# Hybrid gMLP and attention trunk on one core: the fourth quadrant of direct pairs moved into the fifth product's bank, seven-product pairs spread over the slab, four of them in layer B

## The chip, the cores and the metric

The kernel runs on one core of a Trainium2 chip. The metric is the device time of one launch in microseconds. Five engines work side by side and meet through semaphores: TensorE (PE in the profile; its weight loads are PEld), VectorE (DVE), ScalarE (ACT), GpSimd (POOL) and SyncE (SP), which here issues all DMAs.

## The reference, cut to what matters

Two residual layers on 256 tokens of width 2048, all in fp32. Nearly all the work is in four weight matrices that are read once each.

```python
def mixer_a(h, w_in, ln_g, ln_b, w_s, b_s, w_out):       # w_in 2048 x 12288, w_out 4096 x 2048
    p = h @ w_in
    uv = jax.nn.gelu(p[..., :2 * A_WIDTH], approximate=False)
    u, v = uv[..., :A_WIDTH], uv[..., A_WIDTH:]
    z = p[..., 2 * A_WIDTH:]
    v = layer_norm(v, ln_g, ln_b)
    mixed = jnp.einsum('gts,bnsgc->bntgc', ws, vc) + b_s.T[None, None, :, :, None]
    return (u * mixed.reshape(b, s, A_WIDTH) * jax.nn.silu(z)) @ w_out

def mixer_b(h, w_in, w_out, slopes):                     # w_in 2048 x 20480, w_out 2048 x 2048
    p = h @ w_in                                         # q, k, v of three groups, and z
    # three dilated causal window attentions, 16 heads of 128, merged by softmax denominators
    return (o * jax.nn.silu(z)) @ w_out

# reference(): x + mixer_a(rms_norm(x)), then x + mixer_b(rms_norm(x)), then a last rms_norm
```

## The kernel before, in words

**Splitting.** TensorE multiplies in a reduced fp32 form, so each fp32 operand is split into a rounded high part and a remainder. `split` (L126) does it with a ScalarE copy (L127) and a VectorE subtraction (L128). `triple` (L196) adds one 128 x 128 by 128 x 512 product to a bank of PSUM with three matmuls: high by high (L198), remainder by high (L199) and high by remainder (L200). The weights are split as they stream in: `load_pair` (L182) brings 256 rows of two chunks of 512 columns, left and right, by two DMAs of 512 KB into a `raw` tile, and the parts go to `wh` and `wl` (four buffers each, `NW`).

**Slabs and pairs.** `slab` (L202) computes 256 tokens by two chunks of columns. The 2048 rows of the sum are taken as eight pairs of blocks of 128. A pair is a 2 x 2 by 2 x 2 product of blocks: four result quadrants, (token half, chunk), called (0, L), (0, R), (1, L), (1, R). A *direct* pair costs eight products, 24 matmuls. A *seven-product* pair uses sums of blocks as Strassen's scheme does (Winograd's form): seven products, 21 matmuls. The sums of the operand are made once for a layer (`Operand.from_full`, L149). The sums of the weights, `tsum`, are made for each pair on VectorE (L247, L249, L250) and are split too, so such a pair has a split of 1536 columns of `raw` and one of 2048 columns of `tsum`, and takes two buffers of `wh` and `wl`.

The first five pairs of a slab are direct and fill four banks; then the bank of (1, R) is copied out by ScalarE (L241), and the last three pairs (`SA`, `SB`) are seven-product ones, which fill seven banks: q1, p5, p6, p7 and the three quadrants left. At the end a ScalarE copy and eight VectorE operations (L276 to L290) combine the banks into the quadrants, and `done` brings each through ScalarE to its tile. Layer A has twelve slabs: four for v, the first of them all direct because its operand is still being made, and eight for u and z. Layer B has twenty: in each of four quarters of the heads three for q and k, two for v and z. The two output projections (a_w_out two slabs of 16 pairs, b_w_out one slab of 8, then single chunks) are all direct.

**Small work.** Transposes, mixing, scores, softmax and values are put off by `later` and taken one at a time by `tick` (L116) between products, so many ticks apart. Each takes a bank of the same eight (`psp`) and must be emptied by ScalarE or VectorE before the bank serves again.

**Order.** The code is written in this order, but a scheduler moves instructions on every engine and picks buffers and banks. Each engine then runs its own list in order, and the DMAs are issued in SyncE's order.

**Buffers.** `wraw` has three `raw` tiles, `wsum` one `tsum` tile. `stp` has 23 tiles of 4 KB a partition for everything else, the layers' split operands among them.

## Time and profile before

| | |
|---|---|
| time, median of 3 runs | 1792.81 us (1789.93 to 1798.74) |
| profiled execution: time | 1792.22 us |
| its span (first to last instruction) | 1790.4 us |
| PE busy | 1754.9 us, 98% |
| PEld busy | 1443.3 us, 81% |
| DVE busy | 1385.2 us, 77% |
| ACT busy | 973.7 us, 54% |
| DMA | 337.5 MB, 188 GB/s, 57% of 16 engines |
| granted TensorE clock | 9 tenths or more in each of 40 slices |

A matmul's busy time is modelled from its start on and overlaps the next one's, so PE's share alone does not say that TensorE runs at its peak; the distance from one start to the next does. The time outside the span is 1.8 us.

### The profile page before, as it was taken

The page shows a single profiled execution, that of the slowest core. Times are in us where ns is not written, and L with a number is a line of the kernel's source. Part 1 is how long each engine was busy: PE and PEld are TensorE (multiplying, and loading weights), DVE is VectorE, ACT ScalarE, POOL GpSimd, SP SyncE. Part 2 cuts the span into 40 slices and gives each one's busy share as a digit, 9 for nine tenths or more (in the row PEclk, how much of TensorE's full clock was granted, in tenths as well). Part 3 has the DMA queues.
Part 4 walks back from the last instruction along what each step waited for, and adds up shares of the span by engine and source line. Part 5 has one row for each costly group of instructions (what it writes and reads, how often), then busy time and mean ns, then how long its engine had stood idle before and what let it go on. Part 6 is the DMA issues. An engine that isn't in the chain of part 4 may idle for free.

```text
span 1790.4 us, 21099 instructions
## 1 busy us (share of the span) xinstructions
PE 1754.9 (98%) x8185; PEld 1443.3 (81%) x8185; DVE 1385.2 (77%) x1291; ACT 973.7 (54%) x903; POOL 5.3 (0%) x9
## 2 busy tenths in 40 slices
PE   8999999999999999999999999999999999999997
PEld 7787778888887888778888888888888888888786
DVE  5688998888889554687788777887878878788743
ACT  5555455555556443555575455754457545566533
POOL 0000000000000000000000000000000000000000
PEclk9999999999999999999999999999999999999999
DMA  8655555655555775655555555555555555555662
GB/s 272 202 185 188 192 193 194 193 190 189 185 186 169 244 238 190 191 176 171 180 176 189 169 171 180 175 190 185 178 188 188 189 181 183 188 188 187 202 234 71
DMA packets 176596, 337.50 MB, mean 189 GB/s; under 512 B 10768, under 2 KB 14832, under 8 KB 176496
## 3 DMA queue, kind: packets, MB, share of 16 engines
q1 hardware_dynamic: 176496, 336.16, 57.1%
q8 instruction: 64, 1.05, 0.2%
q14 instruction: 36, 0.29, 0.0%
HBM read 330.35 MB, written 5.77 MB: 188 GB/s over the span
## 4 chain that ended last, share of the span: by engine, by line
PE 73%; DVE 13%; issue 6%; ACT 5%; DMA 2%; SPq 0%; POOL 0%; ACTq 0%; DVEq 0%; POOLq 0%
PE acc L200 23%; PE acc L199 22%; PE acc L198 22%; DVE wl L128 7%; ACT wh L127 4%; DVE tsum L247 2%; DVE tsum L250 1%; DVE tsum L249 1%; PE po L666 1%; PE po L668 1%; PE sc L596 1%; PE pp L609 1%; PE sc L590 1%; PE pm L462 1%; DMA raw<-in_b_w_in_dram 1%
## 5 line engine op out<-in xcount | busy, mean ns | idle before, releaser
L128 DVE TENSOR_TENSOR wl<-raw,wh 128x2048 fp32r<-128x2048 f32 (+2 forms) x308 | 636.5, 2068 | 121.9 <-ACT wh L127 121.8
L127 ACT CAST wh<-raw 128x2048 fp32r<-128x2048 f32 (+2 forms) x308 | 531.3, 1736 | 318.0 <-PE acc L199 192.1
L198 PE MATMUL acc<-wh,bh 128*128 128x512 f32 x980 | 395.2, 403 | 2.2 <-ACT full L171 2.2
L199 PE MATMUL acc<-wh,bl 128*128 128x512 f32 x980 | 384.5, 392 | 0.0
L200 PE MATMUL acc<-wl,bh 128*128 128x512 f32 x980 | 384.3, 392 | 0.0
L128 DVE TENSOR_TENSOR wl<-tsum,wh 128x2048 fp32r<-128x2048 f32 x93 | 213.0, 2291 | 193.1 <-ACT wh L127 193.1
L127 ACT CAST wh<-tsum 128x2048 fp32r<-128x2048 f32 x93 | 177.7, 1910 | 312.6 <-DVE tsum L250 156.1
L198 PE MATMUL acc<-wh,ah 128*128 128x512 f32 x603 | 238.8, 398 | 2.3 <-ACT ah L127 2.1
L200 PE MATMUL acc<-wl,ah 128*128 128x512 f32 x603 | 234.9, 392 | 1.5 <-DVE wl L128 1.5
L199 PE MATMUL acc<-wh,al 128*128 128x512 f32 x603 | 236.2, 392 | 0.1
L198 PEld LDWEIGHTS acc<-wh,bh 128*128 128x128 f32 x980 | 184.3, 188 | 41.0 <-ACT full L171 2.4
L200 PEld LDWEIGHTS acc<-wl,bh 128*128 128x128 f32 x980 | 184.0, 188 | 38.8
L199 PEld LDWEIGHTS acc<-wh,bl 128*128 128x128 f32 x980 | 184.5, 188 | 34.5
L200 PEld LDWEIGHTS acc<-wl,ah 128*128 128x128 f32 x603 | 113.4, 188 | 26.5 <-DVE wl L128 2.7
L198 PEld LDWEIGHTS acc<-wh,ah 128*128 128x128 f32 x603 | 113.4, 188 | 26.1 <-ACT ah L127 2.7
L199 PEld LDWEIGHTS acc<-wh,al 128*128 128x128 f32 x603 | 113.7, 189 | 23.7 <-DVE al L128 1.0
L247 DVE TENSOR_TENSOR tsum<-raw 128x1024 f32<-128x1024 f32 x93 | 113.2, 1218 | 4.0 <-DMA raw<-in_a_w_in_dram 3.1
L198 PE MATMUL acc<-wh,gh 128*128 128x512 f32 x256 | 100.1, 393 | 0.7 <-ACT gh L127 0.7
L199 PE MATMUL acc<-wh,gl 128*128 128x512 f32 x256 | 99.9, 390 | 0.4 <-DVE gl L128 0.4
L200 PE MATMUL acc<-wl,gh 128*128 128x512 f32 x256 | 98.9, 390 | 1.3 <-DVE wl L128 1.3
L198 PE MATMUL acc<-wh,bsh 128*128 128x512 f32 x240 | 94.5, 394 | 0.0
L199 PE MATMUL acc<-wh,bsl 128*128 128x512 f32 x240 | 93.6, 390 | 0.0
(197 smaller groups left out, 1976.2 us busy)
## 6 DMA issues: line engine op xcount, KB each, us to landing
raw<-in_b_w_in_dram SPq DMA_DIRECT2D x320, 512.0 KB, 4.6
raw<-in_a_w_in_dram SPq DMA_DIRECT2D x188, 512.0 KB, 4.6
raw<-in_a_w_out_dram SPq DMA_DIRECT2D x56, 512.0 KB, 4.8
raw<-in_b_w_out_dram SPq DMA_DIRECT2D x8, 1024.0 KB, 5.1
raw<-in_b_w_out_dram SPq DMA_DIRECT2D x12, 512.0 KB, 6.2
...
```

The source lines that it names most:

```text
L127: nc.scalar.copy(out=hi, in_=src)
L128: nc.vector.tensor_tensor(out=lo, in0=src, in1=hi.bitcast(F32), op=ALU.subtract)
L198: nc.tensor.matmul(acc, a[0], wh, start=start, stop=False)
L199: nc.tensor.matmul(acc, a[1], wh, start=False, stop=False)
L200: nc.tensor.matmul(acc, a[0], wl, start=False, stop=stop)
L247: nc.vector.tensor_tensor(out=tsum[:, 0:2, :], in0=raw[:, 0:1, :].broadcast_to([P, 2, CW]), in1=raw[:, 1:3, :], op=ALU.add)
L249: nc.vector.tensor_tensor(out=tsum[:, 2, :], in0=tsum[:, 0, :], in1=raw[:, 2, :], op=ALU.add)
L250: nc.vector.tensor_tensor(out=tsum[:, 3, :], in0=tsum[:, 2, :], in1=raw[:, 3, :], op=ALU.add)
L462: nc.tensor.matmul(pm[:, f, t, :], v[:, t, fs], wsT[:, i, :], start=True, stop=True)
L590: nc.tensor.matmul(sc[:, b, :], q[:, i, b * P : (b + 1) * P], k[:, i, :], start=True, stop=True)
L596: nc.tensor.matmul(sc[:, b, :], q[:, i, bs], k[:, i, bs], start=True, stop=True)
L609: nc.tensor.transpose(pt[:, j, :], Sh[:, b, j * P : (j + 1) * P], ident)
```

## The change

Three things change in `slab`.

1. A direct pair's products go to the banks of the seven-product scheme: (0, L) to p2, (1, L) to p4, (1, R) to p5. The bank p5 enters both right quadrants, so (0, R) gets what it lacks by a product with the difference of the two token halves, put into p3. No bank and no copy for (1, R) is left over, so direct and seven-product pairs can stand in any order.
2. Two strings give each pair's kind and two tuples the order in which pairs are taken. Layer A has three seven-product pairs in all twelve slabs (before: none in the first slab), taken as D D D S D S S D. Layer B has four in each slab (before: three), taken as D S D S S D S D. Once the last seven-product pair is done, `early` reads q1, p6 and p7 out, and a direct pair is still to come.
3. The operands keep the blocks that a pair needs, differences included, in tiles of 13 blocks in a pool of their own (`opp`, eight tiles). Layer A's first group of rows is made by `first_group`.

Around it: `tsum` shares the `raw` pool, now four tiles; `stp` has 11 tiles; a_w_out's operand is split in both of its slabs, a group ahead, and only the very first slab splits its first pairs in halves; v is normalised on ScalarE instead of VectorE; the last chunk's weights use `wh` and `wl`; y shares tiles with x3; 11 instead of 4 idle matmuls stand after the first transposes.

```diff
-WARM2 = 4
-NST = 23
+WARM2 = 11
+NST = 11
 NW = 4
-NRAW = 3
-
-SA = 3
-SB = 3
-LOOK = 1
+NRAW = 4
+KINDS_A, ORDER_A = "DDDSDSDS", (0, 1, 2, 3, 4, 5, 7, 6)
+KINDS_B, ORDER_B = "DSDSDSDS", (0, 1, 2, 3, 5, 4, 7, 6)
...
-    wsum = ctx.enter_context(tc.tile_pool(name="wsum", bufs=1))
+    opp = ctx.enter_context(tc.tile_pool(name="opp", bufs=8))
...
+        def sums(self, kg, f, n):
...
+                if kinds[i] == "D":
+                    h = q.rearrange("p (k t) m -> p k t m", t=NT)
+                    tt(out=sf[:, m : m + 2, :], in0=h[:, :, 0, :], in1=h[:, :, 1, :], op=ALU.subtract)
...
+                else:
+                    a11, a21, a12, a22 = (q[:, b, :] for b in range(4))
+                    for o, i0, i1 in ((0, a21, a22), (1, a11, sf[:, m]), (2, a21, a11), (3, a12, sf[:, m + 1])):
+                        tt(out=sf[:, m + o, :], in0=i0, in1=i1, op=ALU.subtract)
...
+            split(sf[:, 0:m, :], self.hi[kg][:, n : n + m, :], self.lo[kg][:, n : n + m, :])
...
-    def slab(h, w, cl, cr, dst, done, s=0, pre=None):
+    def slab(h, w, cl, cr, dst, done, pre=None, fine=0):
...
+        def eight(j):
+            if not h.seven:
+                return [((t, side), (j, t), side) for t in range(NT) for side in (L, R)]
+            return [("p2", (j, 0), L), ("p4", (j, 1), L), ("p5", (j, 1), R), ("p3", ("d", j), R)]
+        seven = (("q1", (0, 0), 0, 1), ("p2", (1, 0), 0, 3), ("p3", "s4", 0, 2), ("p6", "s2", 1, 2),
+                 ("p7", "s3", 1, 1), ("p5", "s1", 1, 0), ("p4", (1, 1), 1, 3))
...
+        def early():
+            nc.scalar.copy(out=c12, in_=acc["q1"])
+            tt(out=c22, in0=acc["p6"], in1=c12, op=ALU.subtract)
+            tt(out=c21, in0=c22, in1=acc["p7"], op=ALU.add)
...
+        for n, i in enumerate(h.order):
...
+            tsum = wraw.tile([P, 4, CW], F32, name="tsum", tag="raw")
...
+            if left["q1"] == 0:
+                early()
...
-        if n > s:
-            nc.scalar.copy(out=dst[R][:, 1, :], in_=acc.pop((1, R)))
...
-        nc.scalar.copy(out=q1, in_=acc["q1"])
-        tt(out=c11, in0=q1, in1=acc[(0, L)], op=ALU.add)
+        tt(out=c11, in0=c12, in1=acc["p2"], op=ALU.add)
         done(0, L, c11)
-        tt(out=u2, in0=acc["p6"], in1=q1, op=ALU.subtract)
-        tt(out=c21, in0=u2, in1=acc["p7"], op=ALU.add)
-        tt(out=u2, in0=u2, in1=acc["p5"], op=ALU.add)
-        if n > s:
-            tt(out=c22, in0=c22, in1=acc["p5"], op=ALU.add)
-            tt(out=c22, in0=c22, in1=c21, op=ALU.add)
-        else:
-            tt(out=c22, in0=c21, in1=acc["p5"], op=ALU.add)
+        tt(out=c12, in0=c22, in1=acc["p5"], op=ALU.add)
+        tt(out=c22, in0=c21, in1=acc["p5"], op=ALU.add)
         done(1, R, c22)
-        tt(out=c12, in0=u2, in1=acc[(0, R)], op=ALU.add)
+        tt(out=c12, in0=c12, in1=acc["p3"], op=ALU.add)
         done(0, R, c12)
-        tt(out=c21, in0=acc[(1, L)], in1=c21, op=ALU.subtract)
+        tt(out=c21, in0=acc["p4"], in1=c21, op=ALU.subtract)
         done(1, L, c21)
...
-            slab(hA, a_w_in[0], AW + c * CW, AW + (c + 1) * CW, v2, v_done, 0 if c == 0 else SA, pre)
+            slab(hA, a_w_in[0], AW + c * CW, AW + (c + 1) * CW, v2, v_done, pre, 2 if c == 0 else 0)
...
-                nc.vector.tensor_scalar(out=v[:, t, :], in0=v[:, t, :], scalar1=mv[:, t, 0:1],
-                                        scalar2=rL[:, t : t + 1], op0=ALU.subtract, op1=ALU.mult)
+                nc.scalar.activation(out=v[:, t, :], in_=v[:, t, :], func=AF.Identity, scale=rL[:, t : t + 1],
+                                     bias=mL[:, t : t + 1])
...
-            if sl == 0 and n == 0:
-                for kg in range(NCH_A - 1):
-                    gA.from_full(kg, gT[kg], False)
-            if sl == 0 and n == AW // P - 2 * KG:
-                gA.from_full(NCH_A - 1, gT[NCH_A - 1], False)
+            if n % KG == 0:
+                for kg in range(2) if n == 0 else (n // KG + 1,):
+                    if kg < NCH_A:
+                        gA.from_full(kg, gT[kg])
...
-    y = [st([P, NT, CW], f"y{c}") for c in range(NQUAD)]
+    y = x3[: NQUAD - 1] + [st([P, NT, CW], "y")]
...
-        for half in range(2):
-            wh = st([P, 2, CW], "fh", F32R)
-            wl = st([P, 2, CW], "fl", F32R)
-            split(raw[:, half * 2 : half * 2 + 2, :], wh, wl)
-            ws += [(kg * KG + half * 2 + j, wh[:, j, :], wl[:, j, :]) for j in range(2)]
+        wh, wl = new_split()
+        split(raw, wh, wl)
+        ws += [(kg * KG + j, wh[:, j, :], wl[:, j, :]) for j in range(KG)]
```

Three places show how the instructions move.

First, VectorE in a slab for q and k of the third quarter of layer B, before: the end of one slab and the first splits of the next. `wl<-raw` of 1536 columns and `wl<-tsum` belong to a seven-product pair, `wl<-raw` of 2048 columns to a direct one; `tmp`, `q` and `k` are the combination of banks; `Sh` is a head's scores.

```order
L128 TENSOR_TENSOR wl_9639<-raw_9631,wh_9638 128x1536
L599 SCALAR_TENSOR_TENSOR Sh_8712<-dm12_83,sc_9568 128x2x128
L128 TENSOR_TENSOR wl_9643<-tsum_9634,wh_9642 128x2048
L128 TENSOR_TENSOR wl_9675<-raw_9667,wh_9674 128x1536
L247 TENSOR_TENSOR tsum_9670<-raw_9667 128x1024
L249 TENSOR_TENSOR tsum_9670<-tsum_9670,raw_9667 128x512
L250 TENSOR_TENSOR tsum_9670<-tsum_9670,raw_9667 128x512
L128 TENSOR_TENSOR wl_9679<-tsum_9670,wh_9678 128x2048
L128 TENSOR_TENSOR wl_9726<-raw_9722,wh_9725 128x2048
L277 TENSOR_TENSOR q_9389<-tmp_9703,acc_9398 128x512
L279 TENSOR_TENSOR tmp_9703<-acc_9616,tmp_9703 128x512
L128 TENSOR_TENSOR wl_9767<-raw_9763,wh_9766 128x2048
```

The same engine, changed, in a slab for q and k of the same quarter: from the end of the combination into the run of two seven-product pairs and the direct pair behind it.

```order
L316 TENSOR_TENSOR q_8775<-acc_8788,q_8775 128x512
L288 TENSOR_TENSOR tsum_9251<-tsum_9251,raw_9246 128x512
L128 TENSOR_TENSOR wl_9250<-raw_9246,wh_9249 128x1536
L289 TENSOR_TENSOR tsum_9251<-tsum_9251,raw_9246 128x512
L287 TENSOR_TENSOR tsum_9293<-raw_9288 128x1024
L288 TENSOR_TENSOR tsum_9293<-tsum_9293,raw_9288 128x512
L289 TENSOR_TENSOR tsum_9293<-tsum_9293,raw_9288 128x512
L128 TENSOR_TENSOR wl_9258<-tsum_9251,wh_9257 128x2048
L128 TENSOR_TENSOR wl_9292<-raw_9288,wh_9291 128x1536
L128 TENSOR_TENSOR wl_9300<-tsum_9293,wh_9299 128x2048
L287 TENSOR_TENSOR tsum_9372<-raw_9367 128x1024
L128 TENSOR_TENSOR wl_9336<-raw_9332,wh_9335 128x2048
```

Three seven-product pairs in a row before the slab's end have become at most two in a row, with a direct pair on either side; the combination follows a direct pair.

Second, TensorE at the program's start, before: `pt` are the transposes of x (`x0` arrives in two halves of columns), `pwarm` the idle matmuls, and the first product ends the fence.

```order
L354 MATMUL pc_112<-ident_80,rows_84 128x16
L176 MATMUL pt_132<-ident_80,x0_105 128x128 x2
L176 MATMUL pt_137<-ident_80,x0_105 128x128 x2
L336 MATMUL pwarm_142<-ones_87 128x128 x4
L176 MATMUL pt_147<-ident_80,x0_105 128x128 x2
L176 MATMUL pt_152<-ident_80,x0_105 128x128 x2
L198 MATMUL acc_157<-wh_124,ah0_130 128x512
```

The same, changed:

```order
L208 MATMUL pt_139<-ident_80,x0_105 128x128 x2
L363 MATMUL pwarm_149<-ones_87 128x128 x11
L231 MATMUL acc_161<-wh_125,ah0_131 128x512
L231 MATMUL acc_165<-wh_125,ah0_131 128x512
L231 MATMUL acc_169<-wh_125,ah0_131 128x512
L232 MATMUL acc_161<-wh_125,al0_132 128x512
L233 MATMUL acc_161<-wl_126,ah0_131 128x512
```

The transposes of the second half of x0 no longer stand ahead of the first products; in the changed list they come after nine products' matmuls and one more.

Third, ScalarE where layer B ends and b_w_out begins, before (`oh0` is the first part of b_w_out's operand, read back from memory into `gl`; `vB2` and `zB` are the last slab's results):

```order
L276 COPY tmp_12108<-acc_12011 128x512
L127 CAST wh_12143<-raw_12138 128x1024
L127 CAST wh_12218<-raw_12213 128x1024
L654 ACTIVATE vB2_11428<-vB2_11428,rB_5335 128x512
L127 CAST wh_12218<-raw_12213 128x1024
L127 CAST wh_12272<-raw_12269 128x2048
L127 CAST oh0_12148<-gl_12123 128x1024
```

The same, changed:

```order
L127 CAST wh_12209<-raw_12206 128x2048
L645 COPY pT_11873<-pp_12135 128x4x128
L127 CAST wh_12259<-raw_12256 128x2048
L127 CAST wh_12311<-raw_12308 128x2048
L689 ACTIVATE vB2_11497<-vB2_11497,rB_5386 128x512
L127 CAST oh0_12214<-gl_12194 128x1024
L127 CAST oh1_12219<-gl_12195 128x1024
```

The casts of the first three pairs now stand ahead of the last slab's results, and `oh0` directly behind the first of these.

## Rows read from the trace of the kernel before

**Rows 1.** The page's first part: span, and each engine's busy time.
```profile
span 1790.4 us, 21099 instructions
PE 1754.9 (98%) x8185; PEld 1443.3 (81%) x8185; DVE 1385.2 (77%) x1291; ACT 973.7 (54%) x903; POOL 5.3 (0%) x9
```

**Rows 2.** Timeline of PE, 59 matmuls in layer B (start, duration, instruction).
```profile
998.74 0.39 PE L199 MATMUL acc<-wh,bl 128*128 128x512 f32 x1
998.74 0.19 PEld L200 LDWEIGHTS acc<-wl,bh 128*128 128x128 f32 x1
...
1011.88 0.39 PE L200 MATMUL acc<-wl,bh 128*128 128x512 f32 x1
```

**Rows 3.** Stages by windows: PE, PEld, DVE, ACT, POOL busy, instructions, PEclk, DMA.
```profile
10.83:62.57 51.74, 49.54 (x221) 39.44 (x219) 35.38 (x34) 35.46 (x49) 0.70 (x1) 0.97 0.80 276
62.57:192.40 129.83, 126.58 (x551) 102.49 (x549) 102.48 (x88) 64.07 (x48) 0.00 (x0) 1.00 0.55 180
192.40:241.16 48.76, 45.00 (x205) 36.42 (x204) 48.08 (x61) 24.18 (x21) 2.14 (x1) 1.00 0.54 178
241.16:513.67 272.51, 271.86 (x1267) 224.18 (x1266) 243.47 (x239) 156.47 (x127) 0.00 (x0) 1.00 0.58 190
559.82:743.68 183.86, 179.94 (x809) 147.82 (x809) 103.83 (x73) 85.68 (x75) 0.00 (x0) 1.00 0.67 216
743.68:1680.27 936.59, 931.01 (x4397) 765.74 (x4397) 753.11 (x694) 535.88 (x510) 1.11 (x1) 1.00 0.55 180
```

**Rows 4.** Groups by line and form: count, busy, mean ns, idle before, releaser.
```profile
L128 DVE TENSOR_TENSOR wl<-raw,wh 128x2048 fp32r<-128x2048 f32 x199 | 454.5, 2284 | 96.0 <-ACT wh L127 96.0
...
L127 ACT CAST wh<-raw 128x2048 fp32r<-128x2048 f32 x199 | 377.2, 1910 | 196.1 <-PE acc L199 93.3 <-DMA raw<-in_b_w_in_dram 37.6 <-DMA raw<-in_a_w_in_dram 21.7
...
L128 DVE TENSOR_TENSOR wl<-tsum,wh 128x2048 fp32r<-128x2048 f32 x93 | 213.0, 2291 | 193.1 <-ACT wh L127 193.1
...
L127 ACT CAST wh<-tsum 128x2048 fp32r<-128x2048 f32 x93 | 177.7, 1910 | 312.6 <-DVE tsum L250 156.1 <-PE acc L199 129.6 <-DVE wl L128 17.3
L128 DVE TENSOR_TENSOR wl<-raw,wh 128x1536 fp32r<-128x1536 f32 x93 | 163.0, 1752 | 11.1 <-ACT wh L127 11.0
L127 ACT CAST wh<-raw 128x1536 fp32r<-128x1536 f32 x93 | 137.8, 1482 | 110.5 <-PE acc L199 91.8 <-DMA raw<-in_b_w_in_dram 6.8 <-issue 6.5
...
L247 DVE TENSOR_TENSOR tsum<-raw 128x1024 f32<-128x1024 f32 x93 | 113.2, 1218 | 4.0 <-DMA raw<-in_a_w_in_dram 3.1 <-DMA raw<-in_b_w_in_dram 0.4
...
L250 DVE TENSOR_TENSOR tsum<-tsum,raw 128x512 f32<-128x512 f32 x93 | 64.0, 689 | 2.1
...
L279 DVE TENSOR_TENSOR tmp<-acc,tmp 128x512 f32<-128x512 f32 x31 | 21.2, 684 | 0.2 <-PE acc L200 0.2
...
L610 ACT COPY pT<-pp 128x512 f32<-128x512 f32 x32 | 18.6, 582 | 19.5 <-PE pp L609 19.5
```

**Rows 5.** Waits in layer B's window (743.68 to 1680.27 us): total, times, longest.
```profile
PEld acc L200 <- DVE wl L128: 8.9, 20, 0.5
```

**Rows 6.** Waits in six u and z slabs (241.16 to 513.67 us).
```profile
PEld acc L200 <- DVE wl L128: 3.6, 7, 0.7
```

**Rows 7.** Timeline of PE: pauses where stages meet (in brackets: idle before, releaser).
```profile
10.42 0.66 PE L176 MATMUL pt<-ident,x 128*128 128x128 f32 x4 [4.26 <-DMA x<-in_x_dram]
...
145.77 0.50 PE L198 MATMUL acc<-wh,ash 128*128 128x512 f32 x1 [1.62 <-ACT wh L127]
...
238.28 0.50 PE L198 MATMUL acc<-wh,ash 128*128 128x512 f32 x1 [2.79 <-ACT wh L127]
...
566.66 1.19 PE L200 MATMUL acc<-wl,gh 128*128 128x512 f32 x4 [1.33 <-DVE wl L128]
...
1680.27 1.78 PE L198 MATMUL acc<-wh,oh 128*128 128x512 f32 x4 [3.42 <-ACT oh L127]
...
1758.09 0.50 PE L198 MATMUL acc<-fh,oh 128*128 128x512 f32 x1 [2.47 <-ACT fh L127]
```

**Rows 8.** Timeline of ACT at the start: the first weight cast.
```profile
6.67 1.04 ACT L127 CAST wh<-raw 128x1024 fp32r<-128x1024 f32 x1 [1.80 <-DMA raw<-in_a_w_in_dram]
```

272 lines of the change are left out of this document (139 added, 133 removed).

## The prediction

> **What bounds the kernel now.** I read the engines' shares first, then the distance of matmuls, then the stages. TensorE is busy for 98% of the span [rows 1], but a matmul's shown time overlaps the next one's, so the share alone proves nothing. The distance does: from the first to the last of 59 consecutive matmuls in layer B are 13.14 us [rows 2], so 58 steps of 0.2266 us, though each shows 0.39 us. A direct pair (24 matmuls) thus takes 5.44 us and a seven-product pair (21) 4.76 us, if nothing waits. The 69 matmuls this change removes are judged by that distance.
>
> Then the stages [rows 3]. In layer B's 20 slabs TensorE is without work for 5.6 of 936.6 us, in six slabs for u and z for 0.6 of 272.5 us. Both are bound by TensorE. VectorE is busy there for 80.4% and 89.3%. The second number matters most: **with VectorE at 89% TensorE still does not pause.** The v slabs (62.57 to 192.40 us) and the first u and z slab pause for 3.3 and 3.8 us, the first slab for 2.2 us, and there are short pauses where stages meet [rows 7].
>
> **The change, part by part.**
>
> *Matmuls removed.* Layer B gets one more seven-product pair in each of 20 slabs, layer A three in the first slab: 23 products, 69 matmuls. At 0.2266 us: 13.6 us in layer B, 2.0 us in the first slab, 15.6 us in all. In layer B that lies on the path, since nothing but TensorE sets the pace there.
>
> *What layer B pays on VectorE and ScalarE.* A pair that becomes seven-product loses a split of 2048 columns (2.284 us) and gains a split of 1536 (1.752), one of `tsum` (2.291) and three additions (1.218 and two of 0.689) [rows 4]: 4.36 us more. One combination of the eight goes (0.684). So VectorE's work per slab rises from 753.11/20 = 37.7 to 41.3 us, while the slab falls from 46.8 to 46.2 us: **89.5% busy**, what the u and z slabs already bear. ScalarE gains 1.482 us net (a cast of 1536 columns): 26.8 to 28.3 us, 61%. The copy of (1, R) becomes that of q1, at the same price. The cover is the two splits' lead that four `wh` and `wl` buffers give; without it the 4.36 us would stand in the open, 20 times. Weight loads wait for VectorE's remainders 8.9 us in 20 slabs now [rows 5], 0.45 us a slab, and 3.6 us in 6 slabs, 0.60 a slab, where VectorE is at 89% [rows 6]. I let layer B rise to that level: 0.15 x 20 = 3 us. The bound from below is nothing (no three pairs in a row any more), from above the whole 13.6 us. Layer B: 13.6 - 3 = **-10.6 us**.
>
> *Banks.* From its second to its seventh pair a layer B slab now holds seven of eight banks, so small tiles share one; before, that was so in the last three pairs. Each of them must be emptied (0.58 us for a copy by ScalarE, [rows 4]) before the next. They come two ticks or more apart, at least four products or 2.7 us. I cost that at nothing; the six slabs for u and z, whose last three pairs already run so without a pause [rows 3], are the cover. At the slab's end the new order helps: the banks of q1, p6 and p7 are read out behind one more direct pair (5.4 us), so the next slab finds four free.
>
> *First slab.* It starts when the first cast ends, 6.67 + 1.04 us [rows 8], not after the second half of x0 (10.42 us, [rows 7]): up to 2.7 us earlier; the 11 idle matmuls stand in the gap before. Against that, VectorE's 35.4 us of 51.7 [rows 3] grow by three pairs (13.1 us), and by my estimate 2 us for operand differences (from the 1.218 us per 1024 columns): 50.5 us, nearly the whole slab. ScalarE grows by 4.4 us and, estimated likewise, 5 us, to 45 us. I set the slab's saved 2.0 us and its early start against that lag: **0**, between -4 and +6.
>
> *v slabs and first u and z slab.* Two of their pauses stand before seven-product matmuls that wait for a cast (1.62 and 2.79 us, [rows 7]), in the run of three such pairs. The run becomes single, then double. I take -2 of the 3.3 us and -1 of the 3.8 us (the normalisation of v now sits on ScalarE, which is half idle): **-3**, between -5 and +2.
>
> *Second half of the u and z work.* VectorE loses the two normalisations and one combination a slab, but TensorE does not wait for it: 0.
>
> *Layer A's output.* Two groups instead of seven are split at its start, where TensorE waits 1.33 us for one [rows 7]: **-1**. The splits made again in the second slab, 8 subtractions of 1024 columns at 1.218 us [rows 4], lie beside its slack (80 of 183.9 us are idle in that window, [rows 3]): 0; uncovered they would cost 10.
>
> *Layer B's end.* The pause of 3.42 us before b_w_out [rows 7] ends with the cast `oh0`, which stands behind the casts of the first pairs and waits for its load. In the changed list it stands right behind the first result. On SyncE's queue three loads `gl` now stand one behind the other, ahead of the fourth pair's second half; they wait for tiles of the last softmax, so a late one would hold that half up. **-2**, between -3 and +3.
>
> *Last chunk.* The pause of 2.47 us [rows 7] waits for the cast of `fh`, whose tiles come free late; the weights now take `wh` buffers as the chunk before frees them: **-2**, between -2.5 and +2.
>
> Sum: -10.6 - 3 - 1 - 2 - 2 = -18.6 us. The profiled execution took 1792.2 us, 0.6 us under the median of the runs. That gives 1773.6 and, for the median, **1774 us**.
>
> **A rule against it.** In layer B, weight loads fill 765.74 of 936.59 us, 82% [rows 3], and a load of 0.19 us per step of 0.2266 us [rows 2] can fill no more than 84%; so I count TensorE as full. The Trainium skill, "Perfetto Trace Analysis", section "Identifying the Most-Contended Engine", says that the share of time in matmuls is no measure of TensorE's headroom and that the share in weight loads is, while for VectorE occupancy is a fair one. Read plainly, TensorE then has 18% left, VectorE at 89.5% would be the most contended engine of layer B, and the 13.6 us would not be gained. That the busy share is no measure agrees with [rows 2]; that the load share shows 18% of room does not, since those steps leave at most 84% to the loads. I side with the distance.
>
> **Rivals.**
>
> *VectorE sets layer B's pace.* This is what that rule would make of it. A chain of subtractions has gaps (cast, then subtraction), and VectorE may saturate at less than 100%. For it: in the v slabs TensorE pauses with VectorE at 79% [rows 3]. Against it: the u and z slabs at 89%. At a saturation of 88% a slab takes 41.3/0.88 = 46.9 us, as now: layer B gains nothing, and the other -8 leave 1784 to 1785 us. At 87% a slab takes 47.5 us, which is +13 us and 1798.
>
> *Slower: the one spare bank.* Place: 36 small tiles in each quarter of layer B, 144 in all, of which most now go through one bank while its emptier stands behind a 2.29 us subtraction or a 1.91 us cast in its engine's list. Price: the mean wait times 144. It cancels the gain at 18.6/144 = 0.13 us, and makes the kernel slower by over 0.5% at 0.19 us. With half a copy (0.29 us) each time it is +42 - 18.6: 1816 us. For it: six of eight pairs instead of three run so, and the emptier's order was fixed without knowing real durations. Against it: the tiles' spacing.
>
> *The first slab lags.* VectorE needs 50.5 us and its first pairs wait for loads: +6 there, 1780 us. Still faster.
>
> **How the numbers follow.** 0.5% (9 us) is about what a measurement of this kernel can tell from no change: under 1783.8 is faster, over 1801.8 slower. Forecast, a lagging first slab included: 0.66, lying between 1764 and 1783, all faster. VectorE sets the pace: 0.21, from 1781 to 1800, a fifth of it (0.04) still faster, the rest the same. The spare bank: 0.13, half of the way up slower (0.11), the rest the same (0.02). So faster 0.70, same 0.19, slower 0.11. The range runs from 1763 to 1795: it leaves out the bank's case and the ends of the others.
>
> **What would show it.** Right: layer B takes about 926 us (46.3 a slab), VectorE near 89% there, matmuls still 0.2266 us apart, and weight loads wait some 12 us for VectorE. The pauses before b_w_out and before the last chunk are under 1.5 us. The prediction is wrong if layer B stays at 936 us or more: then either waits of L233 for VectorE's remainder lead (VectorE sets the pace), or matmuls of small tiles such as `pp`, `sc` and `tq` wait for ScalarE or VectorE (the bank). If layer B gains its 10 us and the total does not, the first slab's end, now at 62.57 us, tells.

## The result, and the profile after

The changed kernel takes **1750.4 us** (median of 4 runs, 1748.9 to 1753.4), the kernel before in the same session 1793.6 us: ratio 0.976, 95% interval 0.973 to 0.979. The forecast was 1774 us, between 1763 and 1795: the sign is right, the size is not. 43 us went instead of 19.

The first part of the page of the changed kernel [rows 1]; its profiled execution took 1750.4 us:

```profile
span 1748.6 us, 21067 instructions
PE 1728.4 (99%) x8130; PEld 1434.7 (82%) x8130; DVE 1460.0 (83%) x1366; ACT 1025.9 (59%) x929; POOL 6.0 (0%) x9
```

The stages after, by windows from the first matmul of a stage to the first of the next (columns: length, then busy us of PE, PEld, DVE, ACT and POOL, granted clock, DMA) [rows 3]:

```profile
7.72:62.64 54.92, 49.42 (x213) 37.76 (x212) 49.81 (x63) 41.69 (x62) 1.80 (x1) 0.97 0.77 263
62.64:187.25 124.61, 124.61 (x552) 103.11 (x550) 112.79 (x95) 68.14 (x50) 0.00 (x0) 1.00 0.62 207
187.25:231.30 44.05, 44.05 (x204) 36.69 (x203) 39.48 (x44) 34.01 (x35) 2.14 (x1) 1.00 0.58 191
231.30:546.42 315.12, 315.12 (x1478) 262.23 (x1477) 279.31 (x273) 187.32 (x145) 0.00 (x0) 1.00 0.59 194
546.42:727.84 181.42, 179.22 (x812) 147.99 (x810) 112.71 (x88) 91.40 (x83) 0.00 (x0) 1.00 0.63 204
727.84:1644.64 916.80, 913.21 (x4337) 757.98 (x4337) 813.98 (x752) 559.61 (x509) 0.80 (x1) 1.00 0.57 186
1644.64:1696.47 51.83, 51.83 (x264) 44.12 (x265) 28.46 (x27) 23.03 (x19) 0.00 (x0) 1.00 0.80 273
1696.47:1718.23 21.76, 21.76 (x97) 18.02 (x96) 13.21 (x11) 9.54 (x13) 0.00 (x0) 1.00 0.27 96
```

Length and PE busy are equal in the v slabs, the u and z slabs, the slab of b_w_out and the chunk behind it: TensorE has no pause left there that these columns show (a matmul is shown with 0.39 us and starts 0.2267 us behind the one before it, so a wait of under 0.16 us stays hidden). The same cuts in the trace of before give the differences:

| stage, us | before | after | difference | forecast |
|---|---|---|---|---|
| up to the end of the first slab | 62.57 | 62.64 | +0.1 | 0 |
| v slabs 2 to 4 | 129.8 | 124.6 | -5.2 | -2 |
| first u and z slab | 48.8 | 44.1 | -4.7 | -1 |
| seven u and z slabs | 318.7 | 315.1 | -3.5 | 0 |
| layer A's output (a_w_out) | 183.9 | 181.4 | -2.4 | -1 |
| layer B, 20 slabs | 936.6 | 916.8 | -19.8 | -10.6 |
| b_w_out, slab | 53.4 | 51.8 | -1.6 | in "layer B's end" |
| b_w_out, both chunks to the last matmul | 49.1 | 44.3 | -4.8 | -2 |

("Layer B's end", -2, lies across the layer B row and the one below.) So the first slab stayed, as forecast, and every other stage gained about twice its forecast or more, the seven u and z slabs where nothing was forecast. Layer B's matmuls are as far apart as before: from 999.77 to 1009.97 us there are 45 steps of 0.2267 us. Their waits went: the 8.9 us that weight loads waited for VectorE's remainders [rows 5], forecast to become 12, are 0.6. Waits in layer B after (total, times, longest):

```profile
ACT wh L127 <- PE acc L232: 139.2, 69, 4.0
ACT wh L127 <- DVE tsum L289: 87.2, 36, 5.8
DVE tsum L287 <- DMA raw<-in_b_w_in_dram: 39.5, 17, 4.2
PEld acc L231 <- ACT oh L127: 2.3, 1, 2.3
PEld acc L233 <- DVE wl L128: 0.6, 3, 0.2
```

ScalarE's casts wait most for a matmul that gives a `wh` tile back, and whoever waits for that is ahead of TensorE. But the totals alone do not tell the two kernels apart. The same two waits before the change:

```profile
ACT wh L127 <- PE acc L199: 191.1, 53, 5.5
ACT wh L127 <- DVE tsum L250: 80.0, 20, 4.8
```

What differs is what follows. Before, each of the 20 waits of [rows 5] stands behind one of these 20 waits for sums, one a slab; after, 36 waits for sums are followed by 3 waits for remainders.

### The profile page after: what moved, and what is told of

It reads as the page before. It is cut to its first block, busy times and chain, and to the rows that moved or that the text cites. A ratio compares the mean times of both kernels' runs of the same rounds, so it can differ in the third digit from the quotient of the medians.

```text
span 1748.6 us, 21067 instructions
## 1 busy us (share of the span) xinstructions
PE 1728.4 (99%) x8130; PEld 1434.7 (82%) x8130; DVE 1460.0 (83%) x1366; ACT 1025.9 (59%) x929; POOL 6.0 (0%) x9
## 4 chain that ended last, share of the span: by engine, by line
PE 88%; DVE 5%; issue 2%; DMA 2%; ACT 2%; SPq 0%; ACTq 0%; DVEq 0%; POOLq 0%; POOL 0%
PE acc L231 27%; PE acc L233 27%; PE acc L232 27%; DVE wl L128 3%; DMA raw<-in_b_w_in_dram 1%; ACT wh L127 1%; PE pm L506 1%; PE sc L631 1%; PE pp L644 1%; PE po L703 1%; PE po L701 1%; PE sc L625 1%; PE tq L615 1%; DVE tsum L287 1%; PE tk L615 1%
## 5 line engine op out<-in xcount | busy, mean ns | idle before, releaser
L128 DVE TENSOR_TENSOR wl<-raw,wh 128x2048 fp32r<-128x2048 f32 (+2 forms) x306 | 633.0, 2069 | 114.9 <-ACT wh L127 112.1
L231 PE MATMUL acc<-wh,bh 128*128 128x512 f32 x1200 | 483.1, 403 | 3.6 <-ACT full L202 2.2
L233 PE MATMUL acc<-wl,bh 128*128 128x512 f32 x1200 | 470.2, 392 | 0.0
L232 PE MATMUL acc<-wh,bl 128*128 128x512 f32 x1200 | 468.6, 390 | 0.0
L127 ACT CAST wh<-tsum 128x2048 fp32r<-128x2048 f32 x116 | 221.7, 1911 | 209.3 <-DVE tsum L289 109.6
L128 DVE TENSOR_TENSOR wl<-tsum,wh 128x2048 fp32r<-128x2048 f32 x116 | 265.4, 2288 | 83.8 <-ACT wh L127 83.0
L231 PE MATMUL acc<-wh,ah 128*128 128x512 f32 x732 | 291.2, 399 | 2.8 <-ACT wh L127 2.8
L232 PE MATMUL acc<-wh,al 128*128 128x512 f32 x732 | 285.9, 391 | 0.7 <-DVE al L211 0.7
L233 PE MATMUL acc<-wl,ah 128*128 128x512 f32 x732 | 284.1, 391 | 2.0 <-DVE wl L128 2.0
L233 PEld LDWEIGHTS acc<-wl,bh 128*128 128x128 f32 x1200 | 225.6, 188 | 49.1 <-DVE wl L128 0.6
L232 PEld LDWEIGHTS acc<-wh,bl 128*128 128x128 f32 x1200 | 226.3, 189 | 43.7
L289 DVE TENSOR_TENSOR tsum<-tsum,raw 128x512 f32<-128x512 f32 x116 | 79.4, 685 | 1.0
L288 DVE TENSOR_TENSOR tsum<-tsum,raw 128x512 f32<-128x512 f32 x116 | 79.3, 683 | 0.8
```

Source lines behind the costliest of these rows:

```text
L127: nc.scalar.copy(out=hi, in_=src)
L128: nc.vector.tensor_tensor(out=lo, in0=src, in1=hi.bitcast(F32), op=ALU.subtract)
L231: nc.tensor.matmul(acc, a[0], wh, start=start, stop=False)
L232: nc.tensor.matmul(acc, a[1], wh, start=False, stop=False)
L233: nc.tensor.matmul(acc, a[0], wl, start=False, stop=stop)
L288: tt(out=tsum[:, 2, :], in0=tsum[:, 0, :], in1=raw[:, 2, :], op=ALU.add)
```

## The experiments

The first theory was the prediction's own remark, made larger: three seven-product pairs in a row made VectorE late, and the spread order cured it. Layer B is given below without its last pause, the one before b_w_out's first matmul, since that turned out to move by itself; "last pause" is its length beyond a matmul's step.

| kernel | pairs in B, order | tiles for raw and sums | layer B | last pause | without it | in all |
|---|---|---|---|---|---|---|
| before | 3, run | 3 + 1 | 936.6 | 3.6 | 933.0 | 1793.6 |
| e5 | 3, run (old kernel) | 4 shared | 939.6 | 4.1 | 935.5 | 1789.6 |
| e6 | 4, run (old kernel) | 3 + 1 | 1018.0 | 0 | 1018.0 | 1867.0 |
| e14, e18 | 4, run (old kernel) | 4 shared | 918.3 | 4.0 | 914.3 | 1769.1 |
| after | 4, spread | 4 shared | 916.8 | 2.1 | 914.7 | 1750.4 |
| e1 | 4, run | 4 shared | 925.1 | 10.0 | 915.2 | 1759.2 |
| e9 | 4, run, old bank rule | 4 shared | 920.7 | 4.9 | 915.8 | 1761.1 |
| e10 | 4, spread, late read-out | 4 shared | 915.3 | 2.3 | 913.0 | 1751.2 |
| e2 | 3, spread | 4 shared | 934.4 | 9.0 | 925.4 | 1771.3 |
| e3, e8 | 4, spread | 3 + 1 | 941.0 | 5.0 | 936.0 | 1788.2 |
| e7 | 4, spread | 3 shared | 936.7 | 2.2 | 934.5 | 1780.2 |
| e13 | 4, run | 3 + 1 | 1008.6 | 11.1 | 997.5 | 1886.3 |
| e15 | 4, spread | 5 shared | 911.2 | 1.1 | 910.1 | 1759.2 |
| e17 | 4, spread | 4, a fifth in B | 913.7 | 3.6 | 910.1 | 1747.2 |
| e11 | 5, spread | 4 shared | 992.0 | 10.3 | 981.8 | 1830.8 |
| e16 | 5, spread | 5 shared | 961.0 | 7.1 | 953.9 | 1816.0 |
| e12 | 5, spread, GpSimd | 4 shared | 1071.5 | 7.9 | 1063.6 | 1922.9 |

The layer B columns come from one profiled execution each (of e8 and e18 for the kernels of e3 and e14), and one thing in them no edit made. In the 3.9 us from layer B's first matmul on, the granted clock is 1.00 in before, e5, e8, e10, e15, e16, e17 and e18, and 0.56 to 0.69 in the others; its 24th matmul then starts 5.3 us after the first, or 7.0. So 1.6 us of any difference can be this clock. e4 (below), which edits nothing in layer B, has 935.1 without its last pause at a clock of 0.65, where before has 933.0. Differences of up to 2 us in this column show nothing.

### e1: the order undone

```diff
-KINDS_B, ORDER_B = "DSDSDSDS", (0, 1, 2, 3, 5, 4, 7, 6)
+KINDS_B, ORDER_B = "DSDSDSDS", (0, 2, 4, 6, 1, 3, 5, 7)
             slab(hA, a_w_in[0], AW + c * CW, AW + (c + 1) * CW, v2, v_done, pre, 2 if c == 0 else 0)
+            hA.order = (0, 1, 2, 4, 6, 3, 5, 7)
```

> The changed kernel with one thing undone: the seven-product pairs stand in one run at the end of the slab again (four in layer B; three in layer A, from the second v slab on). Same matmuls, same VectorE work. Theory (the run of such pairs is what made TensorE wait: each of them needs 6.6 us of VectorE, 1.75 + 2.29 + 1.22 + 2 x 0.69, for 4.76 us of TensorE, so a run falls behind by 1.9 us a pair): small waits come back. v1 to v3 go from 124.6 to about 130 us, the first u and z slab from 44.1 to 47 or more, the seven others from 315.1 to 317 to 320, layer B from 916.8 to between 924 (what three in a row lost before, 0.37 us a slab) and 962 (1.9 us a slab more): 1767 to 1810 us in all. Rival (the order within the slab does not matter; the shared pool for the sums, the normalisation on ScalarE or the early read-out brought the gain): within 3 us of the changed kernel's 1750 us.

1759.2 us, ratio to before 0.981 (0.979 to 0.983). v slabs 2 to 4 take 125.1, the u and z slabs 44.1 and 315.2 us: nothing came back. In layer B 0.5 us did, which shows nothing, and one pause before b_w_out:

```profile
PEld acc L231 <- ACT oh L127: 10.2, 1, 10.2
```

The first theory falls. The cast of the first `oh`, on ScalarE's list, now stands behind all the activations of `vB` and `zB` instead of behind the first of `vB` alone (timeline of ScalarE), and TensorE waits for it.

### e2: three pairs in layer B, spread

```diff
-KINDS_B, ORDER_B = "DSDSDSDS", (0, 1, 2, 3, 5, 4, 7, 6)
+KINDS_B, ORDER_B = "DDDSDSDS", (0, 1, 2, 3, 4, 5, 7, 6)
```

> The changed kernel with three instead of four seven-product pairs in layer B, spread as in layer A. Adds 60 matmuls to layer B, takes 4.4 us of VectorE from each slab. Theory (TensorE sets the pace, nothing else in B is late): 60 x 0.2266 = 13.6 us come back, layer B 930.4 us, 1764 us in all; so spreading alone is worth 6 us in layer B (936.6 before). Rival (with four VectorE already holds TensorE up): less than 9 us come back, layer B under 926 us.

1771.3 us, ratio 0.988 (0.986 to 0.989): 21 us came back, more than either theory said. 6.9 of them are the last pause (9.0 for 2.1 us) and 2.5 the slab of b_w_out behind it. In layer B itself the fourth pair is worth 925.4 - 914.7 = 10.7 us: 13.6 for its matmuls, less 2.9 of waits. The prediction had -13.6 + 3 for it, the 3 as waits for remainders. These are 0.6 us in the changed kernel and none in e2, so that the sum comes out is chance.

### e3 and e8: the sums in a tile of their own again

```diff
-NRAW = 4
+NRAW = 3
+    wsum = ctx.enter_context(tc.tile_pool(name="wsum", bufs=1))
-            tsum = wraw.tile([P, 4, CW], F32, name="tsum", tag="raw")
+            tsum = wsum.tile([P, 4, CW], F32, name="tsum", tag="tsum")
```

> The changed kernel with the sums in a pool of their own with one tile, and three tiles for the raw weights, as before the change (same memory). Theory (the spread order makes the second tile unnecessary): within 3 us of 1750 us, no pause in v1 to v3. Rival (the single tile of sums held the next pair's sums up until the last subtraction had read it, and that was the wait that went): 5 to 15 us come back, v1 to v3 at 43 us a slab instead of 41.5, layer B 924 us or more.

> The kernel of e3 once more, for a profile by stages. Theory (the single tile of sums): the 38 us lie in waits of matmuls for VectorE's remainders and ScalarE's casts in all slabs with seven-product pairs: 12 u, z and v slabs and 20 of layer B, about 1.2 us a slab, with the first slab and both output stages unchanged. Rival (loads): the waits end with a DMA of raw weights.

e3: 1788.2 us, ratio 0.997 (0.996 to 0.998): **38 of the 43 us are back**, 4.5 of them in the last pause (5.0 for 2.1 us) and the slab behind it (53.4 for 51.8), which move in other kernels too. By stages (e8) v slabs 2 to 4 take 129.4, the u and z slabs 45.6 and 319.6, layer B 941.0 us; layer A's output and the chunks stay at 181.4 and 44.3. Waits in layer B (one line more in the code: L128 is the cast, L129 the subtraction):

```profile
ACT wh L128 <- DVE tsum L290: 199.0, 56, 7.7
PEld acc L234 <- DVE wl L129: 13.8, 36, 0.9
PEld acc L232 <- ACT wh L128: 13.7, 22, 1.6
ACT wh L128 <- PE acc L233: 2.2, 2, 1.7
```

The wait for a buffer is down from 139.2 to 2.2 us. Casts now wait for the sums, and TensorE for casts and remainders. That is the rival of e3 in kind; it allowed 5 to 15 us. By the durations of [rows 4] a single tile chains the three additions (2.6 us), the cast (1.91) and the subtraction (2.29), 6.8 us from one pair's sums to the next, where TensorE needs 4.76.

### e4: three side edits in the old kernel

```diff
-                nc.vector.tensor_scalar(out=v[:, t, :], in0=v[:, t, :], scalar1=mv[:, t, 0:1],
-                                        scalar2=rL[:, t : t + 1], op0=ALU.subtract, op1=ALU.mult)
+                nc.scalar.activation(out=v[:, t, :], in_=v[:, t, :], func=AF.Identity, scale=rL[:, t : t + 1],
+                                     bias=mL[:, t : t + 1])
...
-            if sl == 0 and n == 0:
-                for kg in range(NCH_A - 1):
+            if sl == 0 and n % KG == 0:
+                for kg in range(2) if n == 0 else (n // KG + 1,):
...
-            wh = st([P, 2, CW], "fh", F32R)
-            wl = st([P, 2, CW], "fl", F32R)
+        wh, wl = new_split()
```

> The kernel before with three side edits of the change alone, each in a stage of its own: the normalisation of v on ScalarE (u and z slabs), the splits for layer A's output group by group, and the last chunk's weights in the wh and wl tiles. Theory: the last 1024 columns of b_w_out fall from 48.9 to about 44.1 us (the pause of 2.47 us and the lower clock behind it go), layer A's output from 183.9 to about 181.5, the u and z slabs stay (48.8 for the first, 318.7 for the others, within 1 us): 1793.5 - 7 = about 1786 us. Rival (the normalisation was what held up the u and z slabs): those fall by 4 to 8 us as well, about 1779 us.

1786.8 us, ratio 0.996 (0.995 to 0.997). The theory holds in the total; in the stages it misses twice. The chunks fall to 44.3 us, as in the changed kernel. The normalisation gives 2.9 us in the first u and z slab (45.9 us) and nothing in the others (319.2). Layer A's output does not move (183.8 us): its 2.4 us have another cause.

### e5, e6, e14 and e18: parts put into the old kernel

e5 and e6; e14 has both edits:

```diff
 e5
-NRAW = 3
+NRAW = 4
-            tsum = wsum.tile([P, 4, CW], F32, name="tsum", tag="tsum")
+            tsum = wraw.tile([P, 4, CW], F32, name="tsum", tag="raw")
 e6
-SB = 3
+SB = 4
```

> The kernel before with one part of the change alone: its one tile for the sums and its three for raw weights become one pool of four (same memory). Same matmuls, same order, three seven-product pairs at the slab's end. Theory after e1 and e3 (what went besides the matmuls was VectorE's remainders coming late because one tile for the sums let it work only one seven-product pair ahead): the waits go here too, layer B from 936.6 to about 930 us, the seven u and z slabs from 318.7 to about 315, v1 to v3 from 129.8 to about 125, about 1780 us in all. Rival (the pool matters only together with the new order or with the early read-out of banks): within 3 us of 1793 us.

> The kernel before with four instead of three seven-product pairs in layer B, at the slab's end, and nothing else (then no direct product needs the copy of the fourth quadrant beside them; 60 matmuls fewer). Theory (the single tile for the sums holds VectorE back, and the fourth pair makes it worse): layer B at 936 us or above, so at least the 13.6 us of the matmuls are lost to waits, 1793 us or more in all. Rival (the fourth pair is worth its matmuls whatever the pools are): layer B about 923 us, 1780 us in all.

> The kernel before with two parts of the change: four seven-product pairs in layer B at the slab's end (e6, 1867 us) and one pool of four tiles for raw weights and sums (e5, 1790 us). Theory (the pool is what lets the fourth pair pay): layer B falls from e6's 1018 us to between 920 and 930, 1770 to 1782 us in all; what is then left to the changed kernel is the last chunk (4.8 us), the normalisation and small things. Rival (the pool is no cure for the run; spreading, banks and read-out are needed too): layer B over 950 us.

> The kernel of e14 once more (1769 us), for its stages. Theory (the pool carries the fourth pair in the old order and with the old bank rule too): layer B between 915 and 930 us (1018 in e6); v1 to v3 at 124.4 and the u and z slabs about 45 and 320 us as in e5; the remaining 19 us to the changed kernel lie in the last chunk (4.8), the u and z slabs (about 5), layer B (about 5) and the output stages. Rival: layer B as in the changed kernel, 915 to 918 us, and the difference lies outside it.

e5: 1789.6 us, ratio 0.998 (0.997 to 0.999). The pool alone takes 5.4 us from v slabs 2 to 4 (124.4), as much as the whole change, and 4.0 from the first u and z slab (44.7), but nothing from the other seven (320.8) or from layer B, so the theory holds in layer A's first stages alone. In layer B the 8.9 us of waits for remainders [rows 5] are gone, all of them, and others have come (here one line less in the code):

```profile
PEld tq L579 <- DVE k L282: 7.8, 11, 1.6
PEld pp L608 <- DVE vB L279: 5.1, 4, 1.5
```

VectorE is further ahead with splits, and its read-out of the banks at a slab's end, for which small tiles `tq` and `pp` wait, stands behind them.

e6: 1867.0 us, ratio 1.041 (1.039 to 1.043), **73 us slower**, as the theory had it. Layer B takes 1018 us. Its waits, and three windows around one pause (it ends at 887.52 us):

```profile
ACT wh L127 <- DVE tsum L250: 91.6, 35, 5.3
PEld acc L198 <- ACT wh L127: 68.6, 21, 4.5
PEld acc L200 <- DVE wl L128: 16.9, 32, 1.3
```

```profile
884.00:887.52 3.52, 0.06 (x1) 0.00 (x0) 1.47 (x4) 2.67 (x3) 0.00 (x0) 0.82 0.27 40
887.52:891.40 3.88, 3.88 (x9) 3.10 (x10) 3.88 (x2) 3.88 (x3) 0.00 (x0) 0.50 0.62 234
891.40:895.30 3.90, 3.90 (x15) 3.10 (x15) 2.85 (x3) 1.47 (x1) 0.00 (x0) 0.79 0.55 157
```

Each slab pauses for the casts of a late sum, and the pause is paid twice: the granted clock is 0.50 in the 3.9 us behind it, half of 2.4 GHz, and 9 and then 15 matmuls start where 17 fit.

e14: 1769.1 us, ratio 0.986 (0.984 to 0.988). Two constants and a pool, and layer B is at 914.3 us without its last pause, as in the changed kernel, **with the old order, the old bank rule and the late read-out**. Parts that gain 4 and lose 73 us alone gain 25 together. e18 (1767.1 us) shows in which stages the other 16 us lie: the chunks (5.0), the seven u and z slabs (5.7), layer A's output (1.9), layer B with its last pause (1.5) and the slab of b_w_out (2.5).

### e7: three tiles, shared

```diff
-NRAW = 4
+NRAW = 3
```

> The changed kernel with a pool of three instead of four tiles for raw weights and sums together. Theory (what counts is that no tile is tied to the sums): less is lost than with the sums apart (e3, 38 us), though there is one tile less: 1755 to 1780 us. Rival (what counts is how many tiles there are for raw weights, that is how far loads run ahead): more than in e3, over 1790 us.

1780.2 us, ratio 0.993 (0.990 to 0.995). With one tile less than in e3, but none tied to the sums, it is 8 us faster than e3, and still 30 us slower than with four. Of the 6.6 us between the profiled executions of e8 and e7, though, 4.5 lie in the last pause and the slab behind it. In layer B without that pause they are 1.5 us apart, the v slabs take 129.5 and the seven u and z slabs 319.4, as in e8. So a fourth tile helps if both uses share it (934.5 to 914.7), and is worth nothing if it is tied to the sums.

### e9 and e10: the bank and the read-out

e9 is e1 with the old bank rule, from the second v slab on (its tail is that of the kernel before, not shown); e10 moves a call:

```diff
 e9
-            return [("p2", (j, 0), L), ("p4", (j, 1), L), ("p5", (j, 1), R), ("p3", ("d", j), R)]
+            return [("p2", (j, 0), L), ("p4", (j, 1), L), ("p8", (j, 1), R), ("p3", (j, 0), R)]
...
+                if own and left["p8"] == 0:
+                    nc.scalar.copy(out=c22, in_=acc.pop("p8"))
 e10
-            if left["q1"] == 0:
-                early()
...
+        early()
         tt(out=c11, in0=c12, in1=acc["p2"], op=ALU.add)
```

> The kernel of e1 (seven-product pairs in one run at the slab's end, pool of four) with the old bank rule, from the second v slab on: the direct pairs' fourth quadrant has a bank of its own, is copied out before the run, and is added in at the end (one VectorE operation of 0.68 us a slab more, the copy of q1 stays). Same matmuls. Theory (once the pool lets VectorE and ScalarE work ahead, small tiles wait for a bank or for their emptier, and the bank saved is what ends that: in e5 matmuls before small tiles lost 11 us in layer B, in e1 3 us): layer B from 925 to 933 us or above, the seven u and z slabs from 315.2 to 318 or above, 1768 us or more in all. Rival (the bank is worth nothing, as the prediction had it): within 3 us of e1's 1759 us.

> The changed kernel with the read-out of q1, p6 and p7 at the slab's end instead of behind the last seven-product pair. Theory (what counts is that at most seven banks are held and that raw weights and sums share four tiles; in e1 the read-out lay at the end too, and only the pause before b_w_out grew): layer B without its last pause within 3 us of the changed kernel's 914.7, u and z slabs unchanged. Rival (the three banks given back a pair earlier are part of the gain, as the prediction supposed): layer B 5 to 15 us longer, with waits where slabs meet.

e9: 1761.1 us, ratio 0.983 (0.981 to 0.984), e10: 1751.2 us, ratio 0.976 (0.975 to 0.978). e9's rival holds: the bank is worth 0.7 us in layer B, which the table cannot tell from nothing. In v slabs 2 to 4 and the u and z slabs it is worth 2.3, 1.0 and 1.3 us, or the extra VectorE operation that comes with the old rule is. A shorter last pause (4.9 for 10.0 us) hides that in the total. The early read-out is worth nothing: e10's theory holds, and the 1.7 us that layer B is shorter there can be the clock behind its first pause (1.00 for 0.60).

### e11, e12 and e16: a fifth seven-product pair

e11's pair needs a larger operand tile; e12 moves an addition, in both layers; e16 is e11 with e15's pools:

```diff
 e11
+KINDS_B, ORDER_B = "DSDSDSSS", (0, 1, 3, 2, 5, 6, 4, 7)
 e12
-            tt(out=tsum[:, 3, :], in0=tsum[:, 2, :], in1=raw[:, 3, :], op=ALU.add)
+            nc.gpsimd.tensor_tensor(out=tsum[:, 3, :], in0=tsum[:, 2, :], in1=raw[:, 3, :], op=ALU.add)
```

> The changed kernel with five instead of four seven-product pairs in layer B (order D S S D S S D S): 60 matmuls fewer, 13.6 us, 45.2 us a slab for TensorE. VectorE needs 40.7 + 4.4 = 45.1 us a slab, as much. Theory (VectorE does not hold TensorE up as long as its work fits, but here nothing is left): VectorE sets the pace, at about the 97% at best that a chain of casts and subtractions allows: 46.5 us a slab or more, layer B 930 us or above, 1763 us or more in all. Rival (VectorE can be filled wholly): layer B 903 to 910 us, about 1740 us.

> The kernel of e11 with the last of the three additions that make the sums on GpSimd: VectorE is rid of 0.69 us a pair, 3.4 us a slab, and needs 41.6 of 45.2 us (92%). Theory (VectorE is what limits e11): layer B 905 to 915 us, 1739 to 1749 us in all, faster than the changed kernel. Rival (GpSimd's addition takes so long, or slows VectorE so much, that the sums come late): layer B no shorter than in e11.

> Five seven-product pairs in layer B (e11) with five tiles in the shared pool. In e11 VectorE was busy 899 of 992 us, 90.7%, and could do no more. Theory (VectorE's ceiling is set by how many pairs can be under way at once, so a tile raises it): layer B 940 to 970 us, VectorE at 93 to 96%, still slower than the changed kernel. Rival (90 to 91% is VectorE's ceiling here, whatever the pools): layer B stays at 990 us. If VectorE could be filled: 905 to 912 us, faster than the changed kernel.

Layer B's windows of e11 and e16:

```profile
730.39:1722.42 992.03, 929.91 (x4277) 747.86 (x4277) 899.47 (x837) 588.99 (x536) 0.69 (x1) 0.99 0.53 174
```

```profile
744.02:1705.06 961.04, 916.73 (x4277) 745.76 (x4277) 895.67 (x838) 584.52 (x536) 1.27 (x1) 1.00 0.55 180
```

e11: 1830.8 us, ratio 1.021 (1.019 to 1.023). Here VectorE is late: casts wait 199.5 us for its sums, weight loads 38.6 us for its remainders and 38.8 us for the casts, and it is busy 899.5 of 992.0 us, 90.7%. That it sets the pace is e11's theory; no run shows the 97% that the expectation gave it. A fifth tile raises the share to 93.2%, as the theory of e16 has it (e16: 1816.0 us, ratio 1.013, 1.011 to 1.014). e12 is the worst of all, 1922.9 us, ratio 1.073 (1.071 to 1.074). Groups of e12:

```profile
L291 POOL TENSOR_TENSOR tsum<-tsum,raw 128x512 f32<-128x512 f32 x136 | 294.3, 2164 | 1493.2 <-DVE tsum L290 1065.2
L127 ACT CAST wh<-tsum 128x2048 fp32r<-128x2048 f32 x136 | 259.5, 1908 | 448.1 <-POOL tsum L291 420.5
```

GpSimd takes 2.16 us for an addition that VectorE does in 0.69 [rows 4], and casts of sums wait 420.5 us for it, as e12's rival had it. VectorE's own subtraction of sums stayed at 2.29 us: the chain was made longer.

### e13: run and own tile together

The edits of e1 and of e3 in one kernel.

> The changed kernel with both undone at once: the seven-product pairs in one run (e1), and the sums in one tile of their own beside three raw tiles (e3). By itself the run cost layer B 0.5 us (without its last pause), the own tile 24 us. Theory (each cures the same lag: a run needs the sums of the next pair while the last are still being read; a spread order has a direct pair between them): together they cost far more than 25 us, layer B 980 us or above, as in e6 (1018 us), 1815 us or more in all. Rival (the two costs add up, and e6 was slow from the old bank rule or the old order of casts): layer B about 942 to 950 us, 1790 us in all.

1886.3 us, ratio 1.052 (1.049 to 1.054). Without the last pause layer B is 82.8 us above the changed kernel, where e1's 0.5 and e8's 21.3 add up to 21.8. The theory holds in layer B: order and pool stand in for each other, and only with neither does the fourth pair ruin it. Another 28 us of the loss lie in the seven u and z slabs (343.1 for 315.1), where the kernel before, with the same run of three pairs and a tile of its own, takes 318.7. What makes them that long here is open.

### e15 and e17: more depth

e15 closes the pool of four with layer A and opens one of five; e17 keeps it and takes every fifth tile in layer B from a pool of one:

```diff
+    def raw_tile(name):
+        extra["n"] += extra["on"]
+        if extra["on"] and extra["n"] % 5 == 0:
+            return extra["pool"].tile([P, 4, CW], F32, name=name, tag="raw")
+        return wraw.tile([P, 4, CW], F32, name=name, tag="raw")
```

> The changed kernel with five instead of four tiles in the shared pool from layer A's output on, where the memory of layer A's mixing is free. Theory (three tiles to four took 22 us from layer B; what is left there to win is 4.6 us of waits for remainders and before small tiles, and 2.1 us before b_w_out): layer B 910 to 917 us, so no more than 7 us faster than the changed kernel. Rival (a wider lead puts small jobs further behind splits, as in e5): layer B 917 to 930 us.

> The changed kernel with a fifth tile for raw weights and sums that is used in layer B only, every fifth time, so that nothing has to wait for it where layer A ends (in e15 that cost 11 us and 2 us; layer B itself fell to 911.2 us). Theory (depth, with about 5 us left to win): layer B 911 to 913 us, the stages ahead of it as in the changed kernel, 1744 to 1747 us in all, faster than both kernels. Rival (the order that the splits get with a fifth tile gives the 5 us back at the end of layer B, as in e1 and e2): 1750 us or more.

Both bring layer B to 910.1 us without its last pause, 4.6 less. e15 loses 11 us where the pools change (1759.2 us, ratio 0.981, 0.979 to 0.983). e17 takes 1747.2 us, ratio 0.974 (0.972 to 0.976). That is 3 us below the changed kernel, but the intervals overlap (0.973 to 0.979): not shown. By stages, 1.6 of the 4.6 us can be the clock behind layer B's first pause (1.00 in both, 0.60 in the changed kernel), 3.0 are given back in e17's last pause and the slab behind it, as its rival had it, and 1.4 of the 3 us in all lie in the first slab, which e17 does not edit.

## Why the prediction missed

*What was missing.* The sum has **no term for the pool**. The text costs matmuls, operands, banks, read-out, casts at the ends; that raw weights and sums now share four tiles stands in the diff and got not even a "nothing". It was the edit that the rest stood on: with it undone 38 of 43 us are lost (e3), in the old kernel it turns the fourth pair from +73 into part of -25 us (e5, e6, e14).

*Matmuls and layer B's waits* (-13.6 + 3). The fourth pair's own price came out: -10.7 us inside the new kernel (e2), with the 3 us in another place than forecast. The step that failed is the base: "weight loads wait 0.45 us a slab now", and "I let layer B rise to that level", 0.60. The waits were read as a matter of VectorE's share, when [rows 5] come from sums that started late. One of the 20 in the trace of before:

```profile
1009.31 2.29 DVE L128 TENSOR_TENSOR wl<-tsum,wh 128x2048 fp32r<-128x2048 f32 x1 [4.11 <-ACT wh L127]
1011.52 1.75 DVE L128 TENSOR_TENSOR wl<-raw,wh 128x1536 fp32r<-128x1536 f32 x1
1013.19 1.22 DVE L247 TENSOR_TENSOR tsum<-raw 128x1024 f32<-128x1024 f32 x1
...
1015.97 1.91 ACT L127 CAST wh<-tsum 128x2048 fp32r<-128x2048 f32 x1 [4.83 <-DVE tsum L250]
1017.91 2.29 DVE L128 TENSOR_TENSOR wl<-tsum,wh 128x2048 fp32r<-128x2048 f32 x1 [2.06 <-ACT wh L127]
...
1020.26 0.30 PEld L200 LDWEIGHTS acc<-wl,bsh 128*128 128x128 f32 x2 [0.48 <-DVE wl L128]
```

With one tile, the next sums begin only behind the subtraction that reads the last; from one such subtraction to the next are 8.6 us, and the weight load waits 0.48 us, though VectorE and ScalarE both stood idle on the way. With the shared pool these waits are gone (e5), in the changed kernel 0.6 us are left, where 12 were forecast, and 933.0 became 925.4 us even at three pairs (e2). The pool alone does not give that in the old kernel (935.5, e5), since small tiles' waits came instead; which other part ends those at three pairs was not separated.

*The rival "VectorE sets the pace"* was right to be there, and its price (a ceiling of 87 to 88%) wrong as a number of its own. In e8 VectorE holds TensorE up at 819.8 of 941.0 us, 87.1%; in the changed kernel it does not at 88.8% (forecast 89.5). The kernel of e18 is at 89.9% (825.1 of 918.3 us) and takes no longer without its last pause (914.3 us). In e11 it stops at 90.7%, with one more tile at 93.2% (e16). So in these runs there is no one ceiling; it moves with the tiles, that is with how many pairs can be under way. The rule weighed in the prediction, from the Trainium skill's "Perfetto Trace Analysis", "Identifying the Most-Contended Engine", reads the changed layer B as bound by VectorE (88.8% against 82.7% in weight loads, 757.98 of 916.80 us). The trace does not agree: TensorE is without work there for 3.6 us of 916.8. What tells is whether a cast's wait for sums reaches a weight load: 0.6 us of waits for remainders in the changed kernel, 13.8 in e8.

*Banks* (0): right in layer B, 0.7 us (e9); at most 4.6 us in layer A. *The spare bank* as a slower case did not come: by the distances of their starts, the steps from a product's matmul to a small tile's lost 1.5 us in all of layer B.

*v slabs and first u and z slab* (-3, measured -9.9). The pauses were found, the cure was misnamed: "the run becomes single, then double" is worth 0.5 us (e1), the pool 5.4 and 4.0, the normalisation 2.9 in the first u and z slab (e5, e4; the last two overlap). *The other u and z slabs* (0, measured -3.5): the step "TensorE does not wait for it" stands against the prediction's own [rows 6]. Behind such waits 16 matmuls of the seven slabs start 0.1 to 0.5 us late, 2.9 us in all, which was passed over because the window shows only 0.6 us without work. Without the fourth tile the time is back (319.6, e8). The pool alone did not give this gain in the old kernel (e5), since transposes then waited for the product of u and z; which further part ends that was not separated.

*Layer A's output* (-1, measured -2.4): splitting group by group is not the cause (e4); what is was not tried. *Layer B's end* (-2): -1.5 for the pause, and -1.6 in the slab behind it, which had no price. That slab takes 51.7 to 51.8 us in all five kernels whose last pause is 2.3 us or less, and 53.3 to 56.5 in all others; the clock behind the pause is shown at the end. It is chance rather than merit: the same pause is 0 to 11 us in the other kernels.

*Last chunk* (-2, measured -4.8): right step, too small. The pause of 2.47 us went (e4 shows it alone), and so did what follows it. The 3.91 us from the first matmul of the last chunk, before and after:

```profile
1758.09:1762.00 3.91, 3.87 (x12) 3.05 (x13) 3.91 (x4) 3.73 (x4) 0.00 (x0) 0.63 0.18 9
```

```profile
1718.23:1722.14 3.91, 3.91 (x19) 3.24 (x18) 2.88 (x3) 3.12 (x5) 0.00 (x0) 1.00 0.00 0
```

12 matmuls at a granted clock of 0.63 became 19 at 1.00. The prediction priced the pause and not the clock behind it.

*First slab* (0, between -4 and +6): +0.1, right. Its first matmul starts 3.1 us earlier (7.72 for 10.83) and from there it takes 3.2 us longer (54.92 for 51.74), VectorE busy 49.8 us where 50.5 were forecast: the start and the lag cancel, as was said.
